# Folding the output gate into w_out and splitting it in the middle of the program, with both parts kept in DRAM

## The chip, the cores and the metric

One core of a Trainium2 chip. The metric is device time in microseconds (us) of one execution of the program. TensorE (PE; its weight loads are PEld), VectorE (DVE), ScalarE (ACT), GpSimd (POOL) and SyncE (SP) each run their own instructions in order and wait for each other through semaphores. DMAs are issued here by SP and by POOL, each from its own queue, also in order.

## The reference

One layer of a decoder trunk, T = D = 1024, all in float32. The input x is normalised and modulated, one large projection feeds two gated linear attention branches, each branch is projected to 1024, and the branches are merged by sigmoid gates. What the change touches are the last lines:

```
shift, scale, gate = jnp.split(c_act @ ada_w[l] + ada_b[l], 3, axis=-1)
...
merged = mg[:, :, 0] * u_h + mg[:, :, 1] * u_g
x = x + gate[:, None, :] * (merged @ w_out[l])
return rms_norm(x, final_norm_w)
```

`gate` is a row of 1024 numbers that multiplies the columns of the output projection's result, so it may as well multiply the columns of `w_out`.

## The kernel before, in words

A float32 product runs as three matmuls of a faster format: each operand is split (`split`, L187) into a high part, a cast on ScalarE (L192), and a low part, a subtract on VectorE (L195), and the product is hi x hi + hi x lo + lo x hi. On-chip data lies in 46 equal slots of 128 x 1024 float32, handed out first in, first out (`Slots`, L34); an instruction that fills a slot waits for the last reader of what lay there. In the profile every slot is called b.

The program runs in stages. From 0 to about 130 us x is normalised. From there to about 830 TensorE works through the projections (L454, and L556 to L558), and the attention of the heads is woven in between as side tracks: generators that yield and are taken up again a few matmuls later, so that a `yield n` says how much of the main work lies between two steps. One such track, `gate_side` (L956), computes the gate row and spreads it over all partitions in `gate_b`, near 632 to 662 us. An attention step that the prediction speaks of goes, in this order: VectorE scales two tiles (L656, L657) and masks the diagonal blocks of the scores (L698); ScalarE copies the scores (L703, L706, L709) and a transposed state (L721); TensorE uses these in L742 and later in L761 and L763.

From about 825 to 1154 come the four last stages, the merge gates' and the branches' projections, each as sums of seven products of quarter matrices (class `Pair`; matmuls at L1313, in the order `PRODUCTS`). Their weights are loaded on SP (L1248), and split on ScalarE (L1255, L1233) and VectorE (L1256, L1234). Results are combined with gates on VectorE (L1300, L1405, L1408) and split once more as the left operand of the output (`make_m`, L192 and L195 at 128 x 512).

The output stage, class `OutBlk` (L1053), ends the program: two halves of 512 columns, eight row tiles each, 24 matmuls per tile (L1083 to L1085). `load` fetches a half of w_out as four blocks of 512 KB on SP (L1063); `prep` splits each (L192 and L195 at 128 x 1024). Behind the matmuls of a tile VectorE multiplies by the gate (L1088), adds x (L1090), ScalarE sums squares (L1092), and VectorE multiplies by the final norm weight (L1095) or, in the second half, finishes the norm; SP stores the result.

Which instruction stands where in an engine's queue is set by a scheduler that takes the program in the written order, which is given by the tracks and by the calls of `after(b, p, i, f)`: f is called ahead of item i of product p of last stage b. Three of these calls belong to the output stage.

Of the kernel before, what the change touches and what calls it, by code (L numbers as in the profile page):

```python
# [10 lines left out]
F32R = mybir.dt.float32r  # L11
# [4 lines left out]
P = 128  # L16
D = 1024
T = 1024
# [64 lines left out]
def hybrid_trunk_kernel(  # L83
# [6 lines left out]
    nc = tc.nc  # L90
# [5 lines left out]
    dp = ctx.enter_context(tc.tile_pool(name="dram", bufs=1, space=bass.MemoryType.DRAM))  # L96
# [3 lines left out]
    S = Slots(sp, N_SLOTS)  # L100
# [86 lines left out]
    def split(src, hi=None, lo=None, eng=None, pin=False):  # L187

        if hi is None:
            hi = S.get(list(src.shape[1:]), F32R)  # L190
            lo = S.get(list(src.shape[1:]), F32R)
        i = nc.scalar.copy(hi, src)  # L192
        if pin:
            tc.keep_in_program_order(i)
        (eng or nc.vector).tensor_sub(lo, src, hi.bitcast(F32))  # L195
        return hi, lo
# [263 lines left out]
    class Feat:  # L460

        raws, parts = 1, 2
# [4 lines left out]
        def load(self):  # L467
            self.lw = load_feat(self.src, self.w)

        def prep(self):  # L470
            self.wt = split_feat(self.lw)
# [484 lines left out]
    def gate_side():  # L956
# [14 lines left out]
        for half in range(2):  # L971
# [3 lines left out]
            nc.tensor.matmul(pg, ones[0:1, :], gbias[0:1, sl], start=False, stop=True)  # L975
            nc.scalar.copy(gate_b[0][:, sl], pg)
        S.free(gacc, gbias)


    h_state = {}  # L980
# [72 lines left out]
    class OutBlk:  # L1053


        def __init__(self, half):
            self.half, self.sl = half, slice(half * 512, half * 512 + 512)

        def load(self):
            self.raw = []  # L1060
            for kk in range(4):
                b = S.get([2, 512])
                nc.sync.dma_start(b, w_out[0, kk * 256:(kk + 1) * 256, self.sl].rearrange("(k p) f -> p k f", p=P))  # L1063
                self.raw.append(b)

        def prep(self):
            self.wt = []
            for b in self.raw:
                self.wt.append(split(b))
                S.free(b)  # L1070

        def run(self, at):
            half, sl = self.half, self.sl
            for n, t in enumerate((4, 5, 6, 7, 0, 1, 2, 3)):
# [9 lines left out]
                    nc.tensor.matmul(po, lh, lo[:, k % 2, :], start=False, stop=False)  # L1084
                    nc.tensor.matmul(po, ll, hi[:, k % 2, :], start=False, stop=(k == KT - 1))  # L1085
                r = xr[t][:, sl]
                tmp = xb_f[:, (n % 2) * 512:(n % 2) * 512 + 512]
                nc.vector.tensor_mul(tmp, po, gate_b[0][:, sl])  # L1088
                R.free(po)
                nc.vector.tensor_add(r, r, tmp)  # L1090
                junk = xb_f[:, 1024 + (n % 2) * 512:1024 + (n % 2) * 512 + 512]
                nc.scalar.activation(junk, r, AF.Square, accum_out=sso[:, t, half:half + 1])  # L1092
                f = fnw[0]
# [355 lines left out]
        fnw[0] = S.get([D])  # L1449
        nc.sync.dma_start(fnw[0], final_norm_w.partition_broadcast(P))  # L1450

    after(3, 6, 3, out0.load)
    after(3, 7, 3, load_norm_w)
    after(3, 4, 1, out0.prep)

    def scores_done():
        while scoring or len(stream.side) > 1:
# [49 lines left out]
        R.lend([pd[:, 0:512], pd[:, 512:1024]])  # L1507
    last_stages()
    make_m()
    out0.run({1: out1.load, 3: out1.prep})  # L1510
    out1.run({})


# [27 lines left out]
```

## Time and profile before

| | |
|---|---|
| time before, median of 3 runs | 1251.12 us (1249.24 to 1251.75) |
| the profiled execution | 1252.38 us, its span 1250.7 us |
| granted TensorE clock, mean | 0.99 |
| w_out before | 8 loads of 512 KB (L1063), first issued at 1122.5, last at 1151.5 us |
| last stages to output, by the first output matmuls | about 1140 to 1154 us |
| last matmul ends | about 1243 us |

Times are counted from the start of the span. In a row of a timeline the first number is the start, the second the duration, then come engine, line, operation and tiles (written <- read), the number of instructions merged into the row, and in brackets the idle time ahead of it with what ended it. A row of waits says which instruction waited for which, the total in us, how many times, and the longest. Rows of stages give the length and then the busy time of each engine with its count.

### The profile page before, as it was taken

How to read it: one execution, taken by the hardware profiler on the slowest of the kernel's cores; microseconds unless marked ns; L12 is line 12 of the kernel's file. 1: busy time of each engine (PE TensorE's matmuls, PEld its weight loads, DVE VectorE, ACT ScalarE, POOL GpSimd, SP SyncE). 2: the span in 40 equal slices, each digit the busy share in tenths (PEclk: the TensorE clock that was granted, in tenths of full speed). 3: DMA queues.
4: the chain of work that ended last, by engine and by line, in shares of the span. 5: the costliest groups of instructions: out<-in, count | busy, mean ns of one | idle time of the engine just before them, and what ended most of it. 6: DMA issues, size and time to landing. Idle time of an engine off the chain costs nothing.

```text
span 1250.7 us, 20782 instructions
## 1 busy us (share of the span) xinstructions
PE 1205.7 (96%) x8603; PEld 999.9 (80%) x8603; DVE 765.2 (61%) x1219; ACT 530.4 (42%) x784; POOL 132.4 (11%) x216
## 2 busy tenths in 40 slices
PE   4799999999999999999999999999999999998997
PEld 3676899989798888788887878877888888787786
DVE  5746425494857556777873365695422668979443
ACT  4467713343334344243332323456643644454222
POOL 5510000201211021021110101011110000000000
PEclk9899999999999999999999999999999999999999
DMA  8832100653644167255251212154546556235202
GB/s 269 278 115 86 52 18 18 217 188 102 203 143 144 63 208 254 92 179 174 96 177 45 60 41 68 38 183 169 173 163 225 179 171 201 83 100 170 118 34 101
DMA packets 126928, 168.82 MB, mean 135 GB/s; under 512 B 7019, under 2 KB 97185, under 8 KB 126834
## 3 DMA queue, kind: packets, MB, share of 16 engines
q1 hardware_dynamic: 115234, 129.53, 33.5%
q0 software_dynamic: 11552, 37.97, 7.8%
q8 instruction: 67, 1.10, 0.4%
q14 instruction: 27, 0.22, 0.1%
q10 hardware_dynamic: 48, 0.01, 0.0%
HBM read 125.53 MB, written 41.94 MB: 134 GB/s over the span
## 4 chain that ended last, share of the span: by engine, by line
PE 59%; issue 24%; DVE 8%; DMA 3%; POOL 2%; ACT 2%; SPq 1%; POOLq 0%; DVEq 0%; ACTq 0%
PE pd L454 13%; PE pd L1313 11%; PE sc_ps L1313 5%; PE pm L1313 5%; PE pd L556 2%; PE pd L557 2%; PE pd L558 2%; DVE scT L250 1%; PE pm L761 1%; PE pm L742 1%; PE pm L763 1%; PE pd L1083 1%; PE pd L1084 1%; PE pd L1085 1%; DVE b L195 1%
## 5 line engine op out<-in xcount | busy, mean ns | idle before, releaser
L454 PE MATMUL pd<-b,b 128*128 128x512 f32 x1632 | 386.3, 393 | 0.0
L454 PEld LDWEIGHTS pd<-b,b 128*128 128x128 f32 x1632 | 302.4, 188 | 64.0 <-issue 0.5
L1313 PE MATMUL pd<-b,b 128*128 128x512 f32 x720 | 175.7, 395 | 2.5 <-DVE b L866 1.5
L1313 PEld LDWEIGHTS pd<-b,b 128*128 128x128 f32 x720 | 134.7, 189 | 35.4 <-DVE b L866 1.9
L195 DVE TENSOR_TENSOR b<-b,b 128x1024 fp32r<-128x1024 f32 (+1 forms) x95 | 101.8, 1082 | 74.7 <-ACT b L192 34.8
L192 ACT CAST b<-b 128x1024 fp32r<-128x1024 f32 (+1 forms) x95 | 84.6, 904 | 104.0 <-DVE b L1169 14.7
L1256 DVE TENSOR_TENSOR b<-b,b 128x1024 fp32r<-128x1024 f32 x56 | 68.3, 1224 | 68.5 <-ACT b L1255 46.6
L1255 ACT CAST b<-b 128x1024 fp32r<-128x1024 f32 x56 | 58.5, 1051 | 62.8 <-PE pd L1313 17.2
L1313 PE MATMUL sc_ps<-b,b 128*128 128x512 f32 x324 | 79.0, 391 | 0.3 <-ACT scT L706 0.3
L1313 PE MATMUL pm<-b,b 128*128 128x512 f32 x300 | 72.5, 389 | 3.4 <-DVE b L1256 3.4
L513 PE MATMUL pd<-b,b 128*128 128x256 f32 x256 | 74.2, 290 | 0.0
L515 PE MATMUL pd<-b,b 128*128 128x256 f32 x256 | 72.5, 283 | 0.0
L514 PE MATMUL pd<-b,b 128*128 128x256 f32 x256 | 72.4, 283 | 0.0
L1313 PEld LDWEIGHTS sc_ps<-b,b 128*128 128x128 f32 x324 | 60.4, 188 | 13.6 <-ACT scT L706 0.8
L1313 PEld LDWEIGHTS pm<-b,b 128*128 128x128 f32 x300 | 56.3, 188 | 15.5 <-DVE b L1256 3.8
L1234 DVE TENSOR_TENSOR b<-b,b 128x1024 fp32r<-128x1024 f32 x36 | 45.1, 1263 | 18.1 <-ACT b L1233 10.3
L1171 POOL DMA_DIRECT2D ws<-b x64 | 34.6, 541 | 194.8 <-DVE b L1165 87.1
L556 PE MATMUL pd<-b,b 128*128 128x512 f32 x128 | 52.0, 406 | 0.0
L557 PE MATMUL pd<-b,b 128*128 128x512 f32 x128 | 50.4, 394 | 0.0
L558 PE MATMUL pd<-b,b 128*128 128x512 f32 x128 | 50.4, 394 | 0.0
L648 ACT COPY xb<-b 128x512 f32<-128x512 f32 x48 | 29.5, 620 | 49.3 <-PE sc_ps L628 26.3
L1233 ACT CAST b<-b 128x1024 fp32r<-128x1024 f32 x36 | 37.2, 1049 | 28.9 <-PE pd L1313 10.1
(268 smaller groups left out, 2041.9 us busy)
## 6 DMA issues: line engine op xcount, KB each, us to landing
b<-in_w_in_dram SPq DMA_DIRECT2D x66, 512.0 KB, 4.0
ws<-b POOLq DMA_DIRECT2D x64, 256.0 KB, 3.0
b<-ws SPq DMA_DIRECT2D x32, 512.0 KB, 4.2
b<-in_x_dram SPq DMA_DIRECT2D x16, 512.0 KB, 5.8
b<-in_ada_w_dram SPq DMA_DIRECT2D x32, 256.0 KB, 6.2
b<-in_w_branch_dram SPq DMA_DIRECT2D x16, 512.0 KB, 4.8
b<-h SPq DMA_DIRECT2D x14, 512.0 KB, 4.2
b<-in_w_in_dram SPq DMA_DIRECT2D x24, 256.0 KB, 3.5
```

The lines of the kernel that those rows point to most:

```text
L192: i = nc.scalar.copy(hi, src)
L195: (eng or nc.vector).tensor_sub(lo, src, hi.bitcast(F32))
L454: nc.tensor.matmul(ps[0:w, th * 512:(th + 1) * 512], a[:, k, 0:w], b[:, th * 512:(th + 1) * 512], start=(k == 0 and n == 0), stop=(k == KT ...
L513: nc.tensor.matmul(o, lh, hi[:, k % 4, :], start=(k == 0), stop=False)
L514: nc.tensor.matmul(o, lh, lo[:, k % 4, :], start=False, stop=False)
L515: nc.tensor.matmul(o, ll, hi[:, k % 4, :], start=False, stop=(k == KT - 1))
L556: nc.tensor.matmul(o, lh, hi[:, k % 2, :], start=(k == 0), stop=False)
L557: nc.tensor.matmul(o, lh, lo[:, k % 2, :], start=False, stop=False)
L558: nc.tensor.matmul(o, ll, hi[:, k % 2, :], start=False, stop=(k == KT - 1))
L1255: nc.scalar.copy(hi, t)
L1256: nc.vector.tensor_sub(lo, t, hi.bitcast(F32))
L1313: nc.tensor.matmul(o, a[:, sl], c, start=(p in (1, 5) and kt == 0 and n == 0), stop=(kt == 3 and n == 2), skip_group_check=True)
```

## The change

A new track `out_weights` follows `gate_side`. For each half and each block of w_out it waits until twelve slots are free, loads the block on SP, multiplies it by the gate row on VectorE, splits it, and stores both parts to DRAM from POOL's queue. The output stage no longer splits: `load` fetches the parts, 16 loads of 512 KB on POOL's queue, in three calls (in the last of the four stages two blocks ahead of item 2 of product 7 and two ahead of item 1 of product 4, which comes last; the four blocks of the second half ahead of the third row tile of the first), and the tile's result is added to x in one operation.

```diff
@@ gate_side
         S.free(gacc, gbias)
+        yield 3
+        yield from out_weights()
+        S.free(gate_b[0])
+
+    wo_d = [[[dp.tile([P, T], F32R, name=f"wo{half}{kk}{part}") for part in range(2)] for kk in range(4)]
+            for half in range(2)]
+
+    def out_weights():
+
+        for half in range(2):
+            sl = slice(half * 512, half * 512 + 512)
+            g = gate_b[0][:, sl].unsqueeze(1).to_broadcast([P, 2, 512])
+            for kk in range(4):
+                while len(S.free_list) < 12:
+                    yield 1
+                b = S.get([2, 512])
+                nc.sync.dma_start(b, w_out[0, kk * 256:(kk + 1) * 256, sl].rearrange("(k p) f -> p k f", p=P))
+                yield 5
+                nc.vector.tensor_mul(b, b, g)
+                parts = split(b)
+                for d, t in zip(wo_d[half][kk], parts):
+                    nc.gpsimd.dma_start(d, t.rearrange("p a f -> p (a f)"))
+                S.free(b, *parts)
+                yield 2
@@ OutBlk
-        def load(self):
-            self.raw = []
-            for kk in range(4):
-                b = S.get([2, 512])
-                nc.sync.dma_start(b, w_out[0, kk * 256:(kk + 1) * 256, self.sl].rearrange("(k p) f -> p k f", p=P))
-                self.raw.append(b)
-
-        def prep(self):
             self.wt = []
-            for b in self.raw:
-                self.wt.append(split(b))
-                S.free(b)
+
+        def load(self, kks=range(4)):
+            for kk in kks:
+                pair = S.get([2, 512], F32R), S.get([2, 512], F32R)
+                for d, t in zip(wo_d[self.half][kk], pair):
+                    nc.gpsimd.dma_start(t.rearrange("p a f -> p (a f)"), d)
+                self.wt.append(pair)
@@ OutBlk.run
                 r = xr[t][:, sl]
-                tmp = xb_f[:, (n % 2) * 512:(n % 2) * 512 + 512]
-                nc.vector.tensor_mul(tmp, po, gate_b[0][:, sl])
+                nc.vector.tensor_add(r, r, po)
                 R.free(po)
-                nc.vector.tensor_add(r, r, tmp)
@@
-    after(3, 6, 3, out0.load)
+    after(3, 7, 2, lambda: out0.load(range(2)))
     after(3, 7, 3, load_norm_w)
-    after(3, 4, 1, out0.prep)
+    after(3, 4, 1, lambda: out0.load(range(2, 4)))
@@
-    out0.run({1: out1.load, 3: out1.prep})
+    out0.run({2: out1.load})
     out1.run({})
```

In the changed file the multiply is L996, the load L994, the store L999, the reload L1088, the output matmuls L1102 to L1104 and the add L1106; what was L1256 is L1273, L1313 is L1330, L1300 is L1317, L1405 and L1408 are L1422 and L1425, L1255 is L1272.

TensorE's rows where the last product of the branches (pm) and the first matmuls of the output (sc_ps, pd_7419) meet. Before, b_9811 is the low part that the last branch split (L1256) writes:

```order
L1313 MATMUL pm_7939<-b_9737,b_9810 128x512
L1313 MATMUL pm_7939<-b_9739,b_9810 128x512
L1083 MATMUL sc_ps<-b_9848,b_9625 128x512
L1083 MATMUL pd_7419<-b_9848,b_9625 128x512
L1313 MATMUL pm_7938<-b_9737,b_9810 128x512
L1313 MATMUL pm_7938<-b_9739,b_9810 128x512
L1313 MATMUL pm_7939<-b_9737,b_9811 128x512
```

And now, where b_9899 is that low part, b_9847 the one of the split ahead of it, b_9873 and b_9874 the reloaded parts wo010 and wo011, and b_9936 and b_9937 wo020 and wo021:

```order
L1103 MATMUL sc_ps<-b_9874,b_9736 128x512
L1104 MATMUL sc_ps<-b_9873,b_9737 128x512
L1102 MATMUL sc_ps<-b_9873,b_9865 128x512
L1103 MATMUL sc_ps<-b_9874,b_9865 128x512
L1104 MATMUL sc_ps<-b_9873,b_9866 128x512
L1102 MATMUL pd_7507<-b_9869,b_9713 128x512
L1102 MATMUL sc_ps<-b_9936,b_9766 128x512
L1103 MATMUL sc_ps<-b_9937,b_9766 128x512
L1104 MATMUL sc_ps<-b_9936,b_9767 128x512
L1102 MATMUL sc_ps<-b_9936,b_9892 128x512
L1330 MATMUL pm_8027<-b_9817,b_9899 128x512
```

The first reader of the last split stands 15 rows later than before, at row 4059 in place of 4044, and output matmuls stand ahead of it.

POOL's rows at the end of the program, the reloads; wo_777 is wo000 (first half, block 0, high part), wo_778 wo001, and so on in order, so wo_781 is wo020:

```order
L1401 DMA gate_7_842<-b_8310 128x512
L1088 DMA b_9874<-wo_780 128x1024
L1088 DMA b_9870<-wo_778 128x1024
L1088 DMA b_9869<-wo_777 128x1024
L1088 DMA b_9873<-wo_779 128x1024
L1088 DMA b_9937<-wo_782 128x1024
L1088 DMA b_9940<-wo_783 128x1024
L1088 DMA b_9936<-wo_781 128x1024
L1088 DMA b_10038<-wo_785 128x1024
```

None of the L1088 rows was there before; their order is the one in which slots are expected to come free.

VectorE's rows in the middle, at the attention step of about 684 to 694 us. Before:

```order
L656 TENSOR_TENSOR b_5827<-b_5827,tot_775 128x16x32
L195 TENSOR_TENSOR b_6479<-b_6368,b_6478 128x1024
L195 TENSOR_TENSOR b_6546<-b_6451,b_6545 128x1024
L656 TENSOR_TENSOR b_5827<-b_5827,tot_775 128x8x64
L657 TENSOR_TENSOR b_5647<-b_5647,tot_775 128x8x64
L698 COPY_PREDICATED blk<-mask_767,sc_ps 128x8x16
L746 COPY b_6336<-pm_6337 128x128
```

And now, where b_6010 is the gate row and b_6476 a block of w_out:

```order
L656 TENSOR_TENSOR b_5843<-b_5843,tot_775 128x16x32
L195 TENSOR_TENSOR b_6445<-b_6227,b_6444 128x1024
L195 TENSOR_TENSOR b_6459<-b_6390,b_6458 128x1024
L996 TENSOR_TENSOR b_6476<-b_6476,b_6010 128x1024
L195 TENSOR_TENSOR b_6520<-b_6476,b_6519 128x1024
L656 TENSOR_TENSOR b_5843<-b_5843,tot_775 128x8x64
L657 TENSOR_TENSOR b_5663<-b_5663,tot_775 128x8x64
L698 COPY_PREDICATED blk<-mask_767,sc_ps 128x8x16
L996 TENSOR_TENSOR b_6770<-b_6770,b_6010 128x1024
L195 TENSOR_TENSOR b_6515<-b_6395,b_6514 128x1024
L746 COPY b_6336<-pm_6337 128x128
```

A multiply of a w_out block and its split stand between the splits and the masking of the scores, and a further multiply behind it. On ScalarE, at the next such step, the cast of a w_out block (b_7016, L192) stands between L709 and L721:

```order
L703 COPY scT<-sc_ps 32x4x32 x4
L706 COPY scT<-sc_ps 64x4x64 x2
L709 COPY scT<-blk 32x8x32 x4
L192 COPY b_7105<-b_7016 128x1024
L721 COPY b_6897<-pm_6898 128x512
L721 COPY b_6897<-pm_6904 128x384
```

Before, L721 followed L709 directly there.

## The prediction, made before the changed kernel ran

> **What bounds the kernel now.** I read the busy time of the engines first, then busy time by stage, then the waits, then the timeline at the place that the waits name.
>
> ```profile
> PE 1205.7 (96%) x8603; PEld 999.9 (80%) x8603; DVE 765.2 (61%) x1219; ACT 530.4 (42%) x784; POOL 132.4 (11%) x216
> 1100.00:1140.00 40.00, 40.00 (x178) 32.73 (x177) 32.89 (x43) 22.86 (x31) 0.00 (x0) 1.00 0.41 132
> 1140.00:1165.00 25.00, 20.90 (x83) 16.23 (x82) 23.69 (x32) 10.21 (x15) 0.00 (x0) 0.93 0.67 239
> 1165.00:1245.00 80.00, 78.08 (x341) 63.15 (x339) 33.46 (x59) 18.92 (x44) 0.00 (x0) 1.00 0.13 51
> 1140.00:1145.00 5.00, 1.75 (x8) 1.07 (x6) 5.00 (x9) 3.20 (x5) 0.00 (x0) 1.00 0.00 0
> 1145.00:1150.00 5.00, 4.79 (x13) 3.58 (x14) 5.00 (x8) 0.62 (x1) 0.00 (x0) 0.66 0.34 103
> ```
>
> The columns of a stage are its length, then PE, PEld, DVE, ACT and POOL busy with counts, the clock, the DMA share and GB/s. TensorE is busy 96% of the span, so only what makes it wait, run slowly or finish late counts. One stage stands out: from 1140 to 1165 it is busy 20.90 of 25 us while VectorE is busy 23.69, and inside it are 5 us in which it worked 1.75. The next 5 us run at a clock of 0.66, and 13 matmuls are recorded there. At the pace of the stage ahead (40.00 us for 178 matmuls, 0.225 us each) 13 take 2.9 us; they held TensorE for 4.79, so the clock cost 1.8 to 1.9 us.
>
> ```profile
> PE pm L1313 <- DVE b L1256: 3.4, 1, 3.4
> PE sc_ps L1083 <- DVE xb L1088: 0.6, 1, 0.6
> 1119.15 0.69 DVE L1300 TENSOR_TENSOR b<-b,sc_ps 128x512 f32<-128x512 f32 x1 [1.15 <-ACT b L1287]
> 1125.35 0.68 DVE L1300 TENSOR_TENSOR b<-b,pd 128x512 f32<-128x512 f32 x1
> 1125.95 0.68 DVE L1408 TENSOR_TENSOR b<-b,b 128x512 f32<-128x512 f32 x1
> 1127.15 1.22 DVE L1256 TENSOR_TENSOR b<-b,b 128x1024 fp32r<-128x1024 f32 x1
> 1128.29 0.69 DVE L1408 TENSOR_TENSOR b<-b,b 128x512 f32<-128x512 f32 x1
> 1143.83 1.22 DVE L1256 TENSOR_TENSOR b<-b,b 128x1024 fp32r<-128x1024 f32 x1
> 1146.77 4.09 DVE L195 TENSOR_TENSOR b<-b,b 128x1024 fp32r<-128x1024 f32 x4
> 1145.11 0.49 PE L1313 MATMUL pm<-b,b 128*128 128x512 f32 x1 [3.36 <-DVE b L1256]
> ```
>
> This is the wait. The last split of a branch weight (L1256) starts at 1143.83, and TensorE stood 3.36 us for it. VectorE had not been idle since 1119.15: back to back, a 512-wide operation takes 0.60 us (1125.35 to 1125.95) and a 1024-wide one 1.14 (1127.15 to 1128.29). The four splits of w_out follow at 1146.77.
>
> **The change, part by part.**
>
> *The end of the branch stage.* Taken out there are eight VectorE splits and eight ScalarE casts. The first four splits come behind the late L1256, so their absence alone does not bring it forward. Two other things do. By the order, the operations from the one that started at 1119.15 (L1300 before, L1317 now) up to the last L1256 (now L1273) are 37 before, four of them 1024 wide, and 35 now, also four: two at 0.60, so it starts about 1.2 us earlier, near 1142.6, and ends near 1143.8. And its first reader on TensorE moves back by 15 matmuls (4044 to 4059 among the TensorE rows), 15 x 0.225 = 3.4 us, because matmuls of the output that are now ready fill in. The first reader was due at 1145.11 - 3.36 = 1141.75, now at 1145.1: about 1.3 us after the split ends. The earlier one (L1273 of b_9847) meets its reader with about 1 us to spare by the same count. So I take all of the stage's loss off: 25 - 20.90 = 4.1 us of waiting (the 0.6 us at L1083 in it, since that wait is for the multiply that goes), and 1.8 of slow clock: **-5.9 us**, at worst -3.5 if a margin is missed by 2 us and the clock stays.
>
> *The end of the program.* One operation stands between the last matmul and the square sum where two stood.
>
> ```profile
> 1243.12 0.69 DVE L1088 TENSOR_TENSOR xb<-pm,b 128x512 f32<-128x512 f32 x1 [1.70 <-PE pm L1085]
> 1243.84 0.69 DVE L1090 TENSOR_TENSOR b<-b,xb 128x512 f32<-128x512 f32 x1
> ```
>
> From start to start 0.72 us goes; I take **-0.6**. The fifteen others lie beside matmuls, 33.46 us of VectorE in 80, and give nothing.
>
> *The reload.* POOL issues sixteen loads of 512 KB, in order, and each waits for a free slot. The first two output matmuls that fill in need parts asked for about 1126.5 and come at 1137.8, so they are covered. The tight one is wo020 (wo_781): its slot is freed by the L1273 of b_9847, which ends at about 1138.5; its first reader stands 77 matmuls behind the group that begins at 1126.6, so at 1144.0.
>
> ```profile
> DMA to landing us min/median/max: 4.2/5.8/7.2
> 1130.00:1135.00 5.00, 5.00 (x24) 4.11 (x23) 5.00 (x9) 1.68 (x2) 0.00 (x0) 1.00 1.03 324
> L1171 POOL DMA_DIRECT2D ws<-b x64: 539/539/573, 297.7 to 606.9; - x64
> ```
>
> The first row is of the w_out loads (L1063) of before. An issue on POOL takes 0.54 us, so wo020 leaves at 1139.0 and lands at 1143.2 to 1146.2, in the median at 1144.8: a wait of 0 to 2.2, 0.8 in the median. But it shares the engines with about six other loads of 512 KB asked for within 3 us (wo021, wo030, three rows of x, the final norm weight). At a full DMA share 324 GB/s were moved, and 7 x 0.524 MB at that rate take 11.3 us, or to 1148.5 if they begin at 1137.2 and all end together: 4.5. Between 0 and 5 I take the value near the median landing with some sharing: **+2.0**.
>
> The trace shows no load on POOL while VectorE is full. The nearest rows are the 64 stores of L1171, issued in 539 ns, at most 573, most of them in a stretch where VectorE was busy 136 of 200 us:
>
> ```profile
> 400.00:600.00 200.00, 198.48 (x1753) 166.15 (x1752) 135.99 (x256) 75.29 (x120) 34.58 (x54) 1.00 0.50 159
> ```
>
> If VectorE's operations held back POOL's issues, some of the 64 would be longer than 573 ns. I add nothing. [...]
>
> *The middle.* Eight blocks are each loaded, multiplied, cast, subtracted and stored. At 1.2 to 1.3 us for each of 16 VectorE operations and 1.05 for 8 casts this is 20 and 8 us of engines that have room. What costs is a waiting instruction in an in-order queue.
>
> ```profile
> 685.70 1.22 DVE L195 TENSOR_TENSOR b<-b,b 128x1024 fp32r<-128x1024 f32 x1
> 689.74 1.23 DVE L195 TENSOR_TENSOR b<-b,b 128x1024 fp32r<-128x1024 f32 x1 [2.83 <-ACT b L192]
> 692.02 0.69 DVE L656 TENSOR_TENSOR b<-b,tot 128x512 f32<-128x512 f32 x1 [1.05 <-PE sc_ps L694]
> 693.23 0.29 DVE L698 COPY_PREDICATED blk<-mask,sc_ps 128x128 f32<-128x128 int32 x1
> 693.61 1.06 ACT L703 COPY scT<-sc_ps 32x128 f32<-32x128 f32 x4 [3.90 <-DVE blk L698]
> 697.00 0.97 ACT L721 COPY b<-pm 128x512 f32<-128x512 f32 x2
> 685.73 0.39 PE L557 MATMUL pd<-b,b 128*128 128x512 f32 x1
> 698.27 1.72 PE L742 MATMUL pm<-b,b 128*128 128x128 f32 x14
> PE pm L742 <- ACT b L721: 0.7, 2, 0.4
> ```
>
> Now a multiply (L996) and the split behind it stand ahead of L656, L657 and L698, and behind L698 stand L703 to L721 on ScalarE and L742 on TensorE. The block's load takes a slot that the L557 of 685.73 reads last, to 686.12. With the landing of 4.2 to 5.8 us it is there at 690.3 to 691.9; multiply, cast and subtract (1.2, 1.05, 1.14) and two 512-wide operations put L698 at 694.9 to 696.5 instead of 693.23, 1.7 to 3.3 later. L721 ends at 697.97 and L742 begins at 698.27, 0.3 of cover, so TensorE waits 1.4 to 3.0: I take **+2.3**.
>
> ```profile
> 758.71 1.64 ACT L709 COPY scT<-blk 32x256 f32<-32x256 f32 x4
> 760.38 0.97 ACT L721 COPY b<-pm 128x512 f32<-128x512 f32 x2
> 761.01 1.83 PE L742 MATMUL pm<-b,b 128*128 128x128 f32 x14
> ```
>
> At the next such place but one cast of w_out stands between L709 and L721; L742 already follows L721 closely, so the cast's 1.0 us shows in full if it runs there: **+1.0** (0 to 2). A third place, L996 ahead of L623 at 674, costs 0.2 (0 to 2.5). Together **+3.5**, 1 to 6. The 4 MB read and 8 MB stored here meet a DMA share of 0.24 and cost nothing:
>
> ```profile
> 600.00:780.00 180.00, 178.88 (x1511) 146.16 (x1510) 104.78 (x188) 60.56 (x95) 13.18 (x12) 0.99 0.24 77
> ```
>
> *The sum.* -5.9 - 0.6 + 2.0 + 3.5 = **-1.0 us**, on the profiled execution of 1252.38 us 1251.4. The median of the three runs lies 1.26 us lower, so on that basis 1251.12 - 1.0 = **1250.1**.
>
> **The rivals.**
>
> *Both costs are hidden.* wo020 lands in 4.2 to 5 us, ahead of its reader, and the multiply at 690 finds its block there. For it: the landing's lower end, and tracks that may start their blocks earlier. Against it: a load behind a slot that TensorE itself frees. -5.9 - 0.6 + 0 + 1.0 = -5.5: **1245.6**.
>
> *The reload takes the place of the wait* (slower). wo020 lands at 1149, 5 us late, because the seven loads share the engines. Since a standstill of 3.4 to 3.8 us was followed by 0.66 of the clock, 1.8 us are paid again: -5.9 - 0.6 + 6.8 + 3.5 = +3.8, **1254.9**. It decides from a landing of about 1147.7 on, when the wait passes 3.7 us and the clock drops. For it: the full DMA share at 1130 to 1135. [...]
>
> *VectorE is late all the same.* Then the change does not do what it should at the end: one of the margins of about 1 us is missed by 2. -3.5 - 0.6 + 2.0 + 3.5 = +1.4, **1252.5**, about the same.
>
> *POOL is starved.*
>
> ```profile
> 1155.00:1160.00 5.00, 5.00 (x24) 4.14 (x23) 3.78 (x6) 2.79 (x5) 0.00 (x0) 1.00 1.00 363
> ```
>
> If loads from POOL wait while VectorE is full, wo020 leaves only in VectorE's first gap, which lay behind 1155 and comes some 4.1 us earlier without the four splits of 1146.77, at 1151, and lands at 1157: 13 us late in place of 2: **1261**. [...]
>
> **How the numbers follow.** The forecast has 0.36, both hidden 0.32, the late reload 0.22, VectorE late 0.07, POOL starved 0.03. About 0.2%, 2.5 us, is what a measurement can tell from no change. Faster by more: the hidden case and a little of the forecast's lower side, 0.34. Slower by more: the late reload, the starved queue and a little of the forecast's upper side, 0.28. Same: 0.38. The likeliest case's own range is 1247.5 to 1253.5. The range of all reaches from the hidden case with nothing paid in the middle (-6.5, 1244.6) to the late reload with a little more in the middle, 1256.
>
> **What would show it.** In the profile of the changed kernel: no wait of 3 us for the branch split (L1273) and a clock near 1.00 from 1140 to 1150; a wait of TensorE for a DMA from wo at L1102 or L1103 of about 2 us (near 0, or over 3.7 with a drop of the clock, decides for a rival); waits at L742 for L721 that add up to some 3 us more; one VectorE operation behind the last matmul. I am wrong if the stage from 830 to 1100, which the change only shuffles, gains or loses more than 2 us, or if POOL's issues are longer than 0.6 us.

## The result, and the profile after

The changed kernel is slower: 1256.44 us in the median of 8 runs (1253.11 to 1260.27) against 1249.9 of 8 runs of the kernel before (1247.04 to 1251.75), a ratio of 1.0059 with a 95% interval of 1.0040 to 1.0078. The forecast was 1250.1, no change, with a range up to 1256.0, so the time lies just outside. As a difference it lies further out: -1.0 us was forecast, with a range up to +4.9 (1256.0 less the 1251.12 that it started from), and +6.5 was measured. The profiled execution took 1260.27 us with a span of 1258.5, 7.8 us longer than the span of before and at the slow end of its eight runs; differences of one microsecond between single profiles are therefore not to be leaned on, and each reading below is one that several profiles share.

First the place where the gain was to be, the stages at the end of the changed kernel (the columns are as in the prediction: length, then PE, PEld, DVE, ACT and POOL busy, clock, DMA share, GB/s):

```profile
1140.00:1165.00 25.00, 20.83 (x85) 16.77 (x84) 17.53 (x27) 5.19 (x8) 3.79 (x8) 0.93 0.77 272
1145.00:1150.00 5.00, 5.00 (x23) 4.13 (x22) 5.00 (x8) 1.10 (x2) 2.10 (x4) 1.00 0.68 208
1150.00:1155.00 5.00, 3.34 (x15) 2.44 (x13) 5.00 (x9) 1.23 (x2) 1.07 (x3) 1.00 1.07 406
1155.00:1160.00 5.00, 2.49 (x7) 1.99 (x8) 2.40 (x4) 0.63 (x2) 0.53 (x1) 0.78 1.13 418
```

Everything stands some 9 us later here than before, so the place where TensorE stopped for the branch split (1141.7 to 1145.1) lies at about 1151 to 1154. TensorE now works on there, until 1153.3. But then it stops for something else: from 1150 to 1160 it works only 5.8 of 10 us, with the DMA engines full, and the clock is 0.78 in the second half of that. From 1140 to 1165 it is busy 20.83 of 25 us, as little as before.

The waits of TensorE in the changed kernel name what was lost (in us, times, longest):

```profile
PE sc_ps L1102 <- DMA b<-wo: 4.2, 1, 4.2
PE pm L742 <- ACT b L721: 2.7, 3, 1.4
PE pd L1330 <- DVE b L866: 2.6, 1, 2.6
PE sc_ps L628 <- DVE tot L631: 2.5, 2, 2.0
PE pd L1330 <- ACT b L1400: 1.8, 2, 1.6
PE pd L1330 <- DVE b L1317: 0.9, 1, 0.9
PE pm L761 <- DVE b L748: 0.7, 1, 0.7
```

The 3.4 us for the branch split (L1256, now L1273) are gone from this list, as forecast. A wait of 4.2 us for a reload from DRAM has come, waits for attention steps (L742, L628, L761) have grown, and so have waits of the branch stages (L1330) for L866, L1400 and L1317, at which the forecast had put nothing. The wait for L866 was there before, but shorter:

```profile
PE pd L1313 <- DVE b L866: 1.5, 1, 1.5
```

To see where the lag grows I put the matmuls of two profiles side by side: both traces hold 8603 TensorE matmul records, and the start of a record in one, less that of the record with the same number in the other, is the lag there. The table gives how the lag against the profile of before changes over seven stretches (named by the times of before); the last column is the difference of the spans.

```
record of before at us  2.5-665 665-782 782-861 861-915 915-1128 1128-1164 1164-1243   span
changed kernel            -2.8    +7.5    +1.9    +3.5     -0.9      -0.5      -0.1    +7.8
changed, again            -4.6    +6.3    +3.9    +5.6     -0.9      -0.5      -0.1    +8.9
middle alone              -3.6    +5.5    -0.6    +0.5     -0.1      +0.2       0.0    +1.7
end alone                 -3.8     0.0    +0.1    +0.4     +0.6      +2.1      -0.1    -1.6
reload on SP              -4.9    +5.0    +3.2    +4.0     -0.8      -6.5      -0.1    -0.5
early reload              -6.8    +7.1    +1.9    +3.7     -0.9      -6.4       0.0    -2.1
gate slot kept            -0.6    +3.4    +1.9    +0.5     -0.3      +1.3      -0.1    +5.4
kept and early            -3.0    +5.4    +1.9    +0.6     -0.3      -1.7      -0.1    +1.9
kept, early, prefetch     -1.2    +6.2    -0.6    +0.2      0.0      -4.9      -0.1    -1.1
fold at the old place     -1.2     0.0    -0.6     0.0     -0.3      +0.2      -0.3    -3.0
middle, DMAs alone        -3.1    -0.7    -0.6    +0.3     +0.2      +1.2       0.0    -2.7
early, GpSimd             -2.9    +2.8    +2.2    +3.2     -0.9      -6.4      -0.1    -2.7
early, GpSimd, late free  -2.7    +2.2    +0.2    +1.4     +0.5      -6.4      -0.1    -5.5
the same, casts too       -2.4    +2.9    -0.6    +0.2     +0.3      -6.4      -0.1    -6.9
```

The first stretch is the same program in all of these up to about 630 us, so its -0.6 to -6.8 is scatter of the executions, and the profile of before is among the slow ones there (it has a stretch at half clock at 661 us, which most others lack). It is left out when kernels are compared. What is behind it differs by kernel in a way that repeats.

### The profile page after: what moved, and what is told of

The parts are those of the page before. It is cut to its first block, busy times and chain, and to the rows that moved or that the text cites. A ratio compares the mean times of both kernels' runs of the same rounds, so it can differ in the third digit from the quotient of the medians.

```text
span 1258.5 us, 20874 instructions
## 1 busy us (share of the span) xinstructions
PE 1207.8 (96%) x8603; PEld 1002.7 (80%) x8603; DVE 762.3 (61%) x1211; ACT 529.8 (42%) x784; POOL 151.2 (12%) x248
## 5 line engine op out<-in xcount | busy, mean ns | idle before, releaser
L1330 PE MATMUL pd<-b,b 128*128 128x512 f32 x720 | 175.2, 394 | 6.2 <-DVE b L866 2.6
L1330 PEld LDWEIGHTS pd<-b,b 128*128 128x128 f32 x720 | 135.1, 189 | 38.0 <-DVE b L866 3.1
L192 ACT CAST b<-b 128x1024 fp32r<-128x1024 f32 (+1 forms) x95 | 85.1, 904 | 140.8 <-DVE b L1425 23.0
L1273 DVE TENSOR_TENSOR b<-b,b 128x1024 fp32r<-128x1024 f32 x56 | 69.6, 1247 | 72.7 <-ACT b L1272 37.7
L1272 ACT CAST b<-b 128x1024 fp32r<-128x1024 f32 x56 | 58.3, 1049 | 61.5 <-PE pd L1330 20.4
L1330 PE MATMUL sc_ps<-b,b 128*128 128x512 f32 x324 | 79.2, 391 | 0.0
L1330 PE MATMUL pm<-b,b 128*128 128x512 f32 x300 | 73.2, 393 | 0.0
L1330 PEld LDWEIGHTS sc_ps<-b,b 128*128 128x128 f32 x324 | 60.3, 188 | 13.3 <-ACT scT L706 0.5
L1330 PEld LDWEIGHTS pm<-b,b 128*128 128x128 f32 x300 | 57.2, 191 | 12.1
```

The source lines that it names most:

```text
L1272: nc.scalar.copy(hi, t)
L1273: nc.vector.tensor_sub(lo, t, hi.bitcast(F32))
L1330: nc.tensor.matmul(o, a[:, sl], c, start=(p in (1, 5) and kt == 0 and n == 0), stop=(kt == 3 and n == 2), skip_group_check=True)
```

## The experiments

Each ratio is of the kernel's runs to the runs of the kernel before on the same chip; the changed kernel's is 1.0059.

**The middle alone.** The kernel before with the new track, its stores not read.

```diff
 (before)
+        yield 3
+        yield from out_weights()
 (output stage, gate multiply and splits at the end as before)
```

> The changed kernel's middle (each block of w_out loaded, multiplied, split, both parts stored to DRAM), with the end of the kernel before (raw w_out loaded, split at the end, gate multiplied behind the matmuls); what is stored is not read. Theory A (the time is lost in three places: 5.2 us at the blocked queues from 660 to 770, 5 us in the stages from 830 to 930 as a consequence of the middle, and 5.6 us at the reload, less 5.9 won at the end and 0.6 at the tail): this keeps the first two and drops the rest, so 8 to 10 us slower than before and some 2 slower than the changed kernel. Rival B (what is lost from 830 to 930 comes from the new end stage's order or from chance): 3 to 5 us slower than before, faster than the changed kernel.

1255.31 us, ratio 1.0047 (1.0034 to 1.0059). The stretch from 665 to 782 loses 5.5, but from 782 to 915 nothing is lost (-0.6, +0.5): theory A falls in that part. In this run the middle's work brings no loss behind 782 with it. Up to there the two programs differ in one line, the freeing of the gate row's slot. The time, 5.9 us above before, is more than rival B said too.

**The end alone.**

```diff
 (changed kernel)
-        yield from out_weights()
-        S.free(gate_b[0])
-                for d, t in zip(wo_d[self.half][kk], pair):
-                    nc.gpsimd.dma_start(t.rearrange("p a f -> p (a f)"), d)
+                for t in pair:
+                    nc.gpsimd.dma_start(t, w_out[0, kk * 256:(kk + 1) * 256, self.sl].rearrange("(k p) f -> p k f", p=P).bitcast(F32R))
```

> The changed kernel's end alone: no work on w_out in the middle, POOL loads sixteen blocks of 512 KB in the output stage, read from w_out itself for both parts, and the gate row is computed but not applied, so the output lacks the gate and takes the raw weight twice. Theory A: the wait for VectorE at the last branch split is gone (-5.9), the tail gives -0.6, the reload costs 2 to 6: -4 to 0 us against before, and nothing lost from 830 to 930. Rival B: the loss from 830 to 930 is there without the middle, +1 to +5 us.

1251.21 us, ratio 1.0013 (1.0000 to 1.0026): slower than A said. Next to nothing (0.5 us) is lost from 665 to 915, against B; but the reload costs more than in the changed kernel:

```profile
PE sc_ps L1099 <- DMA b<-in_w_out_dram: 3.5, 1, 3.5
PE sc_ps L1100 <- DMA b<-in_w_out_dram: 2.9, 2, 2.0
```

That is 6.4 us. Here the gate row's slot is not freed, and the loads of the parts have one slot less to go to. They also read w_out itself, in shorter rows, and their issue takes 0.70 us in place of 0.53, so the slot is not the only difference; the run with the slot kept, below, is the cleaner test of it.

**The reload on SP's queue, and the reload asked for earlier.** Two ways to be rid of the wait for wo.

```diff
 (changed kernel; on SP)
-                    nc.gpsimd.dma_start(t.rearrange("p a f -> p (a f)"), d)
+                    nc.sync.dma_start(t.rearrange("p a f -> p (a f)").bitcast(F32), d.bitcast(F32))
 (changed kernel; early)
-    after(3, 7, 2, lambda: out0.load(range(2)))
+    after(3, 6, 3, lambda: out0.load(range(2)))
-    after(3, 4, 1, lambda: out0.load(range(2, 4)))
+    after(3, 7, 2, lambda: out0.load(range(2, 4)))
```

> The changed kernel with the sixteen reloads on SP's queue in place of POOL's. Theory C (the path through POOL makes wo020 late: its loads took 7.1 us in the median): landings come down to the 4 to 6 us of other loads and the wait of 4.2 us and the clock drop behind it fall to 0 to 2, 3 to 5 us faster than the changed kernel. Theory D (wo020 is late because it is asked for late, when its slot comes free, and shares the DMA engines with the loads beside it): the wait stays at 3 us or more, the time within 2 us of the changed kernel.

> The changed kernel with the two calls that load the first half's parts one step earlier (two blocks where the kernel before loaded w_out, two where the changed kernel has the first two). Theory D (asked for late): the wait for wo at the first output matmuls goes, 4 to 6 us faster than the changed kernel, which leaves about +1 us against before. Theory C (slow path through POOL): the landing stays over 7 us but hidden, so the same gain; what tells C from D is the run with the loads on SP. Rival E (slots are so short that the earlier call only moves the wait to the loads of the last branch weights): no gain, a new wait at L1330.

On SP 1252.09 us, ratio 1.0017 (1.0006 to 1.0028); early 1251.96, ratio 1.0020 (1.0007 to 1.0034): both some 5 us faster than the changed kernel. In both the wait for wo is gone and the stretch from 1128 to 1164 gives -6.5 and -6.4. Theory D had said that the wait would stay on SP, so by the times alone theory C had this run right. Landing times decide between their reasons. Of the changed kernel (first row), of the run on SP (second) and of the early run (third), from issue to landing:

```profile
DMA to landing us min/median/max: 3.5/7.1/10.6
```

```profile
DMA to landing us min/median/max: 4.9/6.9/8.9
```

```profile
DMA to landing us min/median/max: 3.6/5.0/11.0
```

A load on SP lands no faster (6.9 against 7.1), and the early loads, still on POOL, land in 5.0, so theory C is wrong in its reason, though its number came out. What SP changes is the order: in its one queue one row of x and the norm weight go ahead, then four parts (1143.9 to 1149.9), and the other seven rows of x come behind those. In the changed kernel POOL and SP ask side by side:

```profile
1145.21 0.34 SPq L137 DMA_DIRECT2D b<-in_x_dram  x1
1145.64 0.38 SPq L1467 DMA_DIRECT2D b<-in_final_norm_w_dram  x1
1146.12 1.01 SPq L137 DMA_DIRECT2D b<-in_x_dram  x2
```

```profile
1146.84 1.09 POOL L1088 DMA_DIRECT2D b<-wo  x2 [9.62 <-PE pm L1330]
1148.96 1.06 POOL L1088 DMA_DIRECT2D b<-wo  x2 [1.03 <-DVE b L1425]
```

```profile
1157.51 0.53 PE L1102 MATMUL sc_ps<-b,b 128*128 128x512 f32 x1 [4.17 <-DMA b<-wo]
```

The part wo020 is the first of the two loads at 1148.96. By then seven loads of 512 KB had been asked for within 4 us (three of x, the norm weight, wo021, wo030 and wo020); with the next one they are 4.2 MB. By the stages above 4.1 MB were moved from 1145.0 to 1157.4 (208 GB/s for 5 us, 406 for 5, 418 for 2.4). The matmul starts at 1157.5. That is theory D's reason, late and shared; what it had not seen is that another queue changes the sharing.

**The gate row's slot kept.**

```diff
 (changed kernel)
         yield from out_weights()
-        S.free(gate_b[0])
```

> The changed kernel without the line that gives the gate row's slot back behind out_weights; nothing else differs. Theory F (the 5 us from 830 to 930 come from that one freed slot: it enters the first-in-first-out list, every slot taken later is another one, and loads, casts and splits of the last four stages come in another order): the waits for L866, L1400 and L1317 there shrink to those of the kernel before, 3.5 to 5 us faster than the changed kernel, about +2 against before. Rival G (they follow from the work and the lag of the middle, or from the new end stage): no change, +6 to +7 against before.

1255.00 us, ratio 1.0049 (1.0032 to 1.0067). In the stretch from 861 to 915 the loss falls to 0.5, from 3.5 and 5.6 in the two profiles of the changed kernel. The waits for L1400 and L1317 shrink as theory F says (waits from 780 to 930 in this run):

```profile
PE pd L1329 <- DVE b L866: 2.4, 1, 2.4
PE pm L877 <- DVE b L195: 0.7, 1, 0.7
PE pd L1329 <- ACT b L1399: 0.3, 1, 0.3
```

(L1329 and L1399 here are L1330 and L1400 there.) The wait for L866 hardly shrinks, and the total is only 1.4 us better than the changed kernel, with intervals that overlap, so the runs' times alone do not tell the two apart. One reason is that without that slot the reload comes later: its waits are 5.4 us in place of 4.2. So F is right on its stretch (861 to 915) and wrong on the total: the same slot that disturbs the stages at 861 helps at 1150.

**Slot kept and early reload; the same with a prefetch in the middle.**

```diff
 (slot kept, early; with prefetch)
-                b = S.get([2, 512])
-                nc.sync.dma_start(b, w_out[0, kk * 256:(kk + 1) * 256, sl].rearrange("(k p) f -> p k f", p=P))
+            b, ahead_b = ahead_b, fetch(*blocks[n + 1]) if n < 7 else None
```

> The changed kernel with the gate row's slot kept and the first half's parts asked for one step earlier. If the three losses are separate and add up, only the middle is left: +4.4 in the middle, -5.9 and -0.6 at the end, together about -2 us against before (-1 to -3.5). If the early loads need the freed slot, a new wait for the loads of the last branch weights shows, and the time is 0 to +3.

> As the run with the slot kept and the loads early, and in the middle the load of each block of w_out is issued one block ahead of its multiply, so that the multiply finds its data. Theory H (the 4.4 us of the middle are multiplies that stand in VectorE's queue and wait for the landing): the waits at L628, L742 and L761 fall back to those of before, 3 to 4.4 us faster than that run, -4 to -6.5 against before. Rival I (it is the work itself ahead of L698 and L721, multiply, cast and subtract): at most 1.5 us of it goes, -2 to -3.5.

1250.74 us, ratio 1.0017 (1.0002 to 1.0032), and 1251.90, ratio 1.0015 (1.0002 to 1.0027). The first is not the -2 of separate losses: a wait for wo of 2.6 us is left, since the kept slot is missed even by the early loads, and 1.9 us are lost from 782 to 861. The second does not decide between H and I, because the prefetch did not bring the blocks in time: the loads asked for earlier wait for slots on SP (two of them 25.9 us in all for a store of wo to end), and the multiply still stands for its block, at the attention step itself for 8.45 us, with L656 right behind it:

```profile
695.95 1.23 DVE L1002 TENSOR_TENSOR b<-b,b 128x1024 f32<-128x1024 f32 x1 [8.45 <-DMA b<-in_w_out_dram]
697.09 0.69 DVE L656 TENSOR_TENSOR b<-b,tot 128x512 f32<-128x512 f32 x1
```

The loss from 665 to 782 is 6.2 against 5.4, with a stretch at half clock in it (some 1.7 us) that the first run does not have. The wait only moves, to L720 behind L656:

```profile
PE pm L720 <- DVE b L656: 2.7, 1, 2.7
PE pm L742 <- ACT b L721: 0.9, 1, 0.9
PE sc_ps L596 <- DVE xb L592: 0.9, 1, 0.9
```

**The gate folded in where the split was.** No DRAM, no move: the multiply stands ahead of the split at the end.

```diff
 (before, prep and run)
             for b in self.raw:
+                nc.vector.tensor_mul(b, b, g)
                 self.wt.append(split(b))
...
-                nc.vector.tensor_mul(tmp, po, gate_b[0][:, sl])
-                nc.vector.tensor_add(r, r, tmp)
+                nc.vector.tensor_add(r, r, po)
```

> The kernel before with the gate folded into w_out where it is split, at the end, without DRAM: eight multiplies of 1024 columns are added just where VectorE is full, sixteen of 512 go behind the matmuls. Theory A (VectorE sets the end of the branch stage, and its multiply behind the matmuls only the tail): the first four multiplies come behind the last branch split, but ahead of the output's operands; 0 to +3 us, with -0.6 at the tail in it. Rival (the multiply behind the matmuls is what costs): -2 us or more.

1249.30 us, ratio 0.9992 (0.9979 to 1.0005): no change that can be measured. The wait of 3.4 us for L1256 stands as before, so the fold by itself is worth no more than the tail. What the change won at the end came from taking the splits out of it, with the order that follows, and not from the gate.

**The middle with its DMAs alone, and the middle on GpSimd.**

```diff
 (middle alone; DMAs alone)
-                nc.vector.tensor_mul(b, b, g)
-                parts = split(b)
+                hi, lo = S.get([2, 512]), S.get([2, 512])
 (changed kernel with early reload; GpSimd)
-                nc.vector.tensor_mul(b, b, g)
-                parts = split(b)
+                nc.gpsimd.tensor_mul(b, b, g)
+                parts = split(b, eng=nc.gpsimd)
```

> The run with the middle alone, without its multiplies, casts and subtracts: each block of w_out is loaded and stored twice, as it is, the same slots are taken, and nothing of it is read later; the end is that of the kernel before. Theory H' (the 4.4 us of the middle are w_out's operations standing ahead of others in the queues of VectorE and ScalarE): the lag from 660 to 770 goes to under 1 us, the time to within 1.5 us of before. Rival J (DMA traffic and slots taken from the attention cost it): 3 us or more stay.

> The changed kernel with the early reload, and with the multiply and the subtract of the middle on GpSimd; TensorE's order is the same as in the run with the early reload alone, VectorE's rows differ by the sixteen operations alone, ScalarE's casts stay. Theory H': of the middle's 4.4 us only what the casts cost stays, 1 to 1.5 us (the wait at L628, and most of those at L742 and L761, go), 3 us faster than with the early reload alone, -0.5 to -1 against before. Rival K (the casts on ScalarE, waiting for the multiply, carry the delay on, and GpSimd is slower): no gain, or slower.

DMAs alone: 1249.97 us, ratio 0.9994 (0.9980 to 1.0008), and the stretch from 665 to 782 loses nothing (-0.7). So 4 MB of loads, 8 MB of stores and the slots cost nothing there, and the whole loss of the middle comes with w_out's operations in the queues of VectorE and ScalarE. On GpSimd: 1248.79 us, ratio 0.9986 (0.9973 to 1.0000), 3 to 4 us faster than the early reload, which was expected to be 3; 2.8 us are lost in the middle in place of 7.1 of the same kernel with VectorE, so more stays than the 1 to 1.5 expected. Neither run separates a multiply that stands in the queue for its block from the length of the work itself: both are gone from VectorE's queue.

**The changed kernel again.** No edit.

> The changed kernel unaltered, again: what of its losses stands in every execution. Expected: +6.5 us against before; the lag from 660 to 770 4.4, or 6 with a clock drop, from 830 to 930 3.5 to 5, and the wait for wo 3 us or more. Rival (the loss from 830 to 930 was chance in one profile): under 2 us there.

1258.43 us, ratio 1.0056 (1.0037 to 1.0075). The wait for wo is 4.2 again, the stretch from 861 to 915 loses 5.6, some of it a stretch at half clock behind the wait for L1400, the middle 6.3. The loss from 830 to 930 was not chance.

**The late free, and the casts on GpSimd too.** Put together from what the runs above showed.

```diff
 (early, GpSimd; late free)
         yield from out_weights()
-        S.free(gate_b[0])
-    after(3, 1, 0, lambda: S.free(rst_h[0]))
+    after(3, 1, 0, lambda: S.free(rst_h[0], gate_b[0]))
 (casts too)
-                parts = split(b, eng=nc.gpsimd)
+                parts = S.get([2, 512], F32R), S.get([2, 512], F32R)
+                nc.gpsimd.tensor_copy(parts[0], b)
+                nc.gpsimd.tensor_sub(parts[1], b, parts[0].bitcast(F32))
```

> As the run with the early reload and GpSimd's multiply and subtract, but the gate row's slot is given back ahead of the last of the four stages (with another tile that is freed there) in place of behind out_weights. Theory F (the freed slot reorders the stages behind it): the stage from 861 to 915 falls from +3.2 to about +0.5, the end keeps its -6.4 if the slot is back in time for the reload: -3 to -5 us against before. If the end needs the slot earlier, a wait for wo comes back, 0 to -2.

> As the run with the late free, with the casts of the middle on GpSimd as well, so that neither VectorE nor ScalarE gets any instruction of w_out in the middle. Theory H' (the queues): the 2.8 us that stayed in the middle go to about 0, and with them the delay at L866 behind it: -5 to -7 us against before. Rival K (GpSimd's own queue now delays the stores of the attention results, L829 and L1043): a new wait on the loads of these, -2 to +1.

1247.29 us, ratio 0.9978 (0.9966 to 0.9991), and 1246.03, ratio 0.9980 (0.9962 to 0.9998): both are faster than the kernel before by about 0.2%, and faster than the changed kernel by 0.8%. The late free brings 861 to 915 from 3.2 to 1.4, without the loss at the end that keeping the slot had. From 782 to 861 the loss falls from 2.2 to 0.2, but 1.7 of these 2.0 are a stretch at half clock (833 to 836) behind a wait of 2.9 us, which does not follow a wait of 2.3 in the other run; that part is not the slot's. The casts were not what was left of the middle: 2.9 with them on GpSimd, 2.2 without, and theory H' does not explain this rest. The last section shows what does.

## Why the prediction was wrong, step by step

In the forecast's own terms the profile of the changed kernel gives -6.4 and -0.7 at the end (-5.9 and -0.6 forecast), 5.9 for the reload (+2.0), 7.5 in the middle (+3.5), and 4.5 in the stages behind the middle (nothing). That is +10.8; the scatter of -2.8 in the first stretch brings it near the 7.8 between the two spans. So one term was missing, and the two that were priced came out about 4 us too low each. Each of the three holds a stretch at half clock, at 680, 837 and 1158 us, of some 1.7 us. The top of the range was too low by the prediction's own bounds: the late reload at 6.8 with the middle at its upper 6 gives +6.3, 1257.4.

**The end of the branch stage: right.** Forecast -5.9, with the tail -0.6. In the five runs without a wait for wo (on SP, early, and the three with GpSimd) the stretch from 1128 to 1164 gives -6.4 or -6.5. The two reasons of the forecast are seen in the changed kernel: the last split starts at 1152.49, which less the lag of 9.3 us is 1143.2 (forecast 1142.6),

```profile
1152.49 1.21 DVE L1273 TENSOR_TENSOR b<-b,b 128x1024 fp32r<-128x1024 f32 x1
```

and no matmul waits for it. In the changed kernel its reader stands behind the wait for wo, which would hide such a wait; the proof is the five runs, in which TensorE waits for nothing there. The tail is one VectorE operation shorter; the span's gain behind the last matmul is 0.7 to 0.8 (-0.6 forecast).

**The reload: the mechanism right, the size wrong.** Forecast +2.0 within 0 to 5; it cost 4.2 us of waiting and a stretch of half clock behind it: -0.5 against -6.4 in the table, 5.9. The issue was forecast for 1139.0 and came, less the lag of 9.3, at 1139.7. The landing was taken near the median of single loads; by the sum of the loads in flight it had been 1148.5 in the prediction itself, and that upper value was the measured one (1157.4 less 9.3 is 1148.1). That it fits to half a microsecond is partly luck: seven loads at 324 GB/s were counted, and it was eight, at 208 GB/s and then over 400. This was the rival of the late reload, which had a chance of 0.22, and the drop of the clock that it names followed. That a wait of 2 us costs no more than its length, as the +2.0 has it, and that the clock drops from a wait of 3.7 us on, were the author's estimates; in these runs the clock fell to half after a wait of 1.96 us, and in the run with the late free it did not after one of 2.3.

**The middle: the place right, the sum too small.** Forecast +3.5 (0.2 at 674, 2.3 at 698, 1.0 at 761). In the changed kernel:

```profile
673.41 1.22 DVE L996 TENSOR_TENSOR b<-b,b 128x1024 f32<-128x1024 f32 x1 [8.97 <-DMA b<-in_w_out_dram]
691.57 1.22 DVE L996 TENSOR_TENSOR b<-b,b 128x1024 f32<-128x1024 f32 x1 [2.78 <-DMA b<-in_w_out_dram]
696.25 0.29 DVE L698 COPY_PREDICATED blk<-mask,sc_ps 128x128 f32<-128x128 int32 x1
```

```profile
678.95 0.89 PE L628 MATMUL sc_ps<-xb,b 128*32 128x48 f32 x64 [1.96 <-DVE tot L631]
700.65 1.83 PE L742 MATMUL pm<-b,b 128*128 128x128 f32 x14 [1.44 <-ACT b L721]
707.32 0.71 PE L761 MATMUL pm<-scT,b 128*128 128x128 f32 x4 [0.72 <-DVE b L748]
679.00:684.00 5.00, 5.00 (x76) 4.05 (x77) 4.18 (x15) 2.70 (x4) 0.00 (x0) 0.66 0.15 42
```

L698 was forecast for 694.9 to 696.5 and ran at 696.25, which less the lag there of 0.6 is 695.6; the waits behind it are 1.44 and 0.72, together 2.2 (2.3 forecast), and L742 waits another 0.91 at 765 (1.0 forecast). The place at 674 was priced at 0.2 and cost 1.96: the multiply stood there for its data until 673.4, VectorE then reached L623 1.1 us after it, and all of that came out at L628. That makes 5.0, within the forecast's 1 to 6, though the place at 674 was mis-sized. Most of the rest of the 7.5 is a stretch at half clock behind the first wait (0.66 from 679 to 684, some 1.7 us), which the forecast had not counted for a wait of 2 us. At 674 and 691 the multiply stood for its block (8.97 and 2.78 us idle), as the prediction had it, and at 765 it was a cast's own length. With no operation of w_out in the queues the loss goes. How much multiply, cast and subtract would cost with the block there in time stays open, since no run had it there in time.

**The stages from 830 to 1100: this is the step that failed.** The prediction put nothing there, and said that it would be wrong if they lost more than 2 us. They lost 5.4 from 782 to 915 in the first profile and 9.5 in the second, 0.9 of it given back later. Nothing in the prediction gives a reason for the zero; it took these stages as only shuffled. For the stretch from 861 to 915 (3.5 and 5.6 us) the cause is a line of the diff that I did not price at all: `S.free(gate_b[0])`. It hands one slot back at about 775 us; the list is first in, first out, so from there on every tile gets another slot, waits for another last reader, and the scheduler writes loads, casts and splits in another order. Of the changed kernel:

```profile
917.21 1.99 ACT L1272 CAST b<-b 128x1024 fp32r<-128x1024 f32 x2 [3.45 <-DMA b<-in_w_in_dram]
919.64 0.57 ACT L1400 ACTIVATE b<-pd 128x512 f32<-128x512 f32 x1
```

```profile
920.27 3.03 PE L1330 MATMUL pd<-b,b 128*128 128x512 f32 x12 [1.55 <-ACT b L1400]
```

Two casts of a weight wait for their load, the gate's activation (L1400) stands behind them on ScalarE, and TensorE waits for that. Five runs free the slot at 775 (the changed kernel twice, on SP, early, GpSimd): 3.2 to 5.6 us lost from 861 to 915. The nine others do not free it, or free it late: 0.0 to 0.6, and 1.4 in one of the two with the late free. The run with the slot kept differs from the changed kernel in that line alone, and the one with the slot kept and the loads early differs in it alone from the early run: 0.5 against 3.5 and 5.6, and 0.6 against 3.7.

From 782 to 861 the line explains less: the changed kernel loses 1.9 and 3.9 us there, the run with the slot kept also 1.9. It is the wait for L866, 1.5 us before, and a stretch at half clock behind it where it is long. Two things lengthen it. In the five runs that free the slot at 775 ScalarE stands idle for 2.5 to 6.0 us ahead of two casts (in all others 1.0 at most at that place), and the activation that L866 needs comes behind these. In the changed kernel the cast waits for a store of yh, the last reader of its new slot:

```profile
831.03 2.00 ACT L1250 CAST b<-b 128x1024 fp32r<-128x1024 f32 x2 [3.88 <-DMA yh<-b]
836.79 5.52 PE L1330 MATMUL pd<-b,b 128*128 128x512 f32 x16 [2.64 <-DVE b L866]
837.00:842.00 5.00, 5.00 (x16) 3.93 (x16) 5.00 (x11) 1.09 (x2) 0.00 (x0) 0.66 0.32 103
```

In the others it goes by which engine comes first. The middle alone (first two rows) and the slot kept (last two) have the same order on TensorE, VectorE, ScalarE and GpSimd up to there. In both an add on GpSimd (L1042) meets VectorE's L598, which stands in the chain ahead of L866:

```profile
818.73 0.62 DVE L598 TENSOR_TENSOR b<-b,b 128x256 f32<-128x256 f32 x1
818.89 2.71 POOL L1042 TENSOR_TENSOR b<-b,b 128x1024 f32<-128x1024 f32 x1
819.86 3.08 DVE L598 TENSOR_TENSOR b<-b,b 128x256 f32<-128x256 f32 x1
820.03 2.41 POOL L1042 TENSOR_TENSOR b<-b,b 128x1024 f32<-128x1024 f32 x1
```

Where VectorE gets through first, in the kernel before and six more, the wait for L866 is 1.4 to 1.5 us; where GpSimd holds it, in the three runs with L598 at 3.05 to 3.08 us, it is 2.3 to 2.4. What decides which goes first these profiles do not show.

**The rivals.** Both costs hidden: refuted, neither was. VectorE late all the same: refuted, no wait for L1273. POOL starved: refuted as put; wo020 was issued in time while VectorE was full, and its issues took 527 to 550 ns. That loads from POOL wait while VectorE is full, on which the 1261 rests, no run shows; loads from SP landed in 6.9 us against 7.1, so here the queue made no difference.

## What to carry to other kernels

Where many transfers were asked for at once, the landing here followed the bytes in flight over the measured rate (wo020 8.4 us after its issue, with 4.2 MB asked for and 208 to 418 GB/s moved), not the median landing of such transfers (5.8 us for w_out's loads before); where the two differ, take the first. In a kernel whose buffers come from a rotating list, taking or freeing one buffer is an edit of everything behind it: price it, or free the buffer behind the stages that it would disturb, as the late free did. A range must hold the sum of the bounds of its own terms. Work moved from a full stretch into one where TensorE is busy is not hidden because the engine that does it has room (VectorE was busy 58% of the time from 600 to 780 us before, and the middle alone lost 5.5 us there, with its DMAs alone -0.7); what counts is who stands behind it in that engine's queue.

## What the runs showed of the hardware

In these runs GpSimd's tensor operations and VectorE's held each other up, one until the other's end, unless VectorE's read a matmul's result. In the run with the casts on GpSimd, VectorE's L632 on 64 columns takes 2.44 us and an L1016 2.62; in the run with the DMAs alone the same two operations (L632 and L1013) take 0.28 and 0.81. Of the first run, VectorE and GpSimd:

```profile
728.54 2.62 DVE L1016 TENSOR_SCALAR b<-b,oml,lb 128x1024 f32<-128x1024 f32 x1 [4.58 <-ACT b L1014]
743.44 2.44 DVE L632 TENSOR_TENSOR tot<-tot 128x64 f32<-128x64 f32 x1
```

```profile
728.22 2.39 POOL L998 TENSOR_TENSOR b<-b,b 128x1024 fp32r<-128x1024 f32 x1
743.37 2.38 POOL L998 TENSOR_TENSOR b<-b,b 128x1024 fp32r<-128x1024 f32 x1
```

and of the second:

```profile
725.99 0.81 DVE L1013 TENSOR_SCALAR b<-b,oml,lb 128x1024 f32<-128x1024 f32 x1 [8.52 <-ACT b L1011]
738.53 0.28 DVE L632 TENSOR_TENSOR tot<-tot 128x64 f32<-128x64 f32 x1
```

Each slow VectorE operation starts 0.1 to 0.3 us after a GpSimd subtract and ends 0.1 to 0.6 us after it. It goes the other way too: GpSimd's add takes 2.40 us alone (710.5 us in the kernel before) and 3.64 where VectorE was first (640.9). Operations of VectorE that read a matmul's result (pm, pd or sc_ps) ran beside GpSimd at their usual length, such as an L1033 at 707.7 with 0.75 us in the run with the casts. The 1.8 us by which L1016 is longer stand again as TensorE's wait of 1.7 us for L592 behind it, and an L656 and an L657 there at 689 to 693 us, of 2.33 and 1.66 in place of 0.69 and 0.68, as its wait of 1.8 us for L721. Against the run with the DMAs alone the middle loses 3.6 us more, and these two waits are nearly all of it.

The clock fell to half (0.50) for 3.4 us after a TensorE wait of 1.96 us (679 to 684 in the changed kernel) and of 2.6 us (837 to 842), and in the kernel before at 661 us with no wait of TensorE at all, in a stretch where 12 matmuls were recorded in 5 us:

```profile
660.00:665.00 5.00, 5.00 (x12) 2.94 (x11) 1.23 (x1) 1.78 (x3) 0.00 (x0) 0.66 0.10 23
```

From 665 us to the last matmul of these profiles it never fell after a single wait of 1.8 us or less, and always after one of 2.4 or more; in between it fell after some (1.9 in the changed kernel's second profile, 2.3 with the slot kept and the loads early) and not after others (2.2 in the run on SP, 2.3 with the late free). Once it fell after two waits of 1.3 us 1.4 us apart (early reload, 833 us). So here a wait of 1.96 us cost its own length and by estimate some 1.7 us more (half of the 3.4).
